# Residual loaded ahead of the products, a third score bank and a new plan in a two-layer decoder trunk

## The chip, the cores and the metric

One core of a Trainium2 chip runs the whole kernel. The metric is the device time of one execution in microseconds. Before the change three runs took 1709.66 to 1713.77 us, with a median of 1711.59 us.

## The reference

The input is x of 2048 positions and 1024 channels in float32. All of it is float32.

```python
# layer 0: gated short convolution
h = rmsnorm(x, norm_a)
B, C, X, G = split(h @ w_in_a, 4)                       # 1024 -> 4 x 1024
y = B * causal_conv3(C * X, conv_a)
x = x + (y * silu(G)) @ w_out_a                         # 1024 -> 1024
# keys and values, once
k, v = split(rmsnorm(x, norm_kv) @ w_kv, 2)             # 8 heads of 64
# layer 1: stick-breaking attention, strictly causal
q, g = split(rmsnorm(x, norm_b) @ w_in_b, 2)
z = q k^T / 8
rev = reverse_cumsum(where(mask, log_sigmoid(-z), 0))   # from the last key backwards
o = exp(where(mask, z + rev, -inf)) @ v
x = x + (o * silu(g)) @ w_out_b                         # 512 -> 1024
return rmsnorm(x, norm_f)
```

## The kernel before

**Layout.** The activations lie transposed, channels on the 128 partitions and positions, last one first, along the free axis, in four chunks c = 0 to 3 of 512 positions. A block is one tile of 128 channels by 512 positions. Every float32 operand of a product is split in a high part (rounded) and a low part (the rest), and a product is three matmuls of these parts (hi·hi, hi·lo, lo·hi).

**Stages.** First the mixer's input products for two blocks of channels, directly (`mixer_in`), then for the rest, two chunks at a time, by Strassen-like units of seven products in place of eight (`fast_unit`): fa, fd and fe are its three PSUM banks, from the tags lin (two banks), z and wt; a product is 12 matmuls of 512 columns. The output products of mixer A follow in the same form, four units of two blocks for chunks 0 and 1 and four for chunks 2 and 3 (`out_unit`, tiles named _o). Then come the K, Q, V and gate products for chunks 0 and 1 as units (kq, vg), and for chunks 2 and 3 directly (pk, pq, pv, pg), the attention of 4 chunks by 8 heads, the output projection (pob) with the final norm, and, for chunk 3, an end (`finish`) that waits for the last head: its last part of the output product (pol), the norm and the store.

**A unit's banks.** In `fast_unit` fa collects a first product; a copy f1 of it is kept, the next product is added onto the bank, and so on, so that the bank passes through several partial sums. Three of these states (f1 and f2 of fa, f5 of fd) are copied by ScalarE to SBUF tiles of the tag ld (5 buffers); TensorE may only go on in the bank once the copy is done. VectorE then adds the other banks onto the copies. The fourth result stays in fa. In `out_unit`, after that, each of the four results gets its residual: a block of x is loaded (tag t, 4 buffers), the result is added onto it (GpSimd for the first block, VectorE for the others), the sum is stored to x1 in HBM, squared by ScalarE and added to a running sum by GpSimd.

**Norms.** The squares are added block by block to one tile; `rstd` sums it over the partitions by matmuls with a column of ones (pst) and takes the root by three steps of Newton on 128 x 4 numbers. `bcast` spreads this factor over the partitions: VectorE multiplies it into four identity matrices (dg) and TensorE multiplies ones by it in float32 (prb). Both tiles come from a bank of their own, tag st.

**Attention.** For each head and chunk of keys: four score tiles (z, 128 queries by 512 keys, two matmuls each, tag z with two banks), a sigmoid on ScalarE, a running product along the keys on VectorE (the scan), transposes on TensorE to a wt bank (two), a split into wth and wtl, and two matmuls with the values into av. The eight PSUM banks are lin 2, z 2, wt 2, av 1, st 1.

**Order.** All instructions are recorded (class `Recorder`), each in a part (mixer unit, output unit, head of a chunk, ...), and put in order before the program is built: PLAN gives each part a start and an end, which become a priority of each of its instructions; then a list scheduler with costs for each engine, buffers and transfers takes the one that can begin first, and among equals the one of the smaller priority. Every engine runs its instructions in that order, and waits in it. Loads and stores are issued from SyncE's queue (SP), keys, values and queries of the attention from ScalarE's.

## Time and profile before

| | us |
|---|---|
| median of the runs | 1711.59 |
| profiled execution | 1716.8 |
| its span, first to last instruction | 1715.0 |
| TensorE busy | 1640.0 |
| VectorE busy | 1346.2 |
| ScalarE busy | 802.3 |
| GpSimd busy | 542.7 |

The profile is of one execution. PE is TensorE's matmuls, PEld its weight loads, DVE VectorE, ACT ScalarE, POOL GpSimd, SPq the queue of SyncE. Since an instruction of TensorE overlaps the next one, a matmul of 512 columns shows about 0.39 us but a row of 12 takes 2.72 us. In a row of the timeline stand the start, the time, engine, operation, output and inputs, and in brackets the idle time before it and what ended it. A row of busy time by stretch has the stretch, its length, then the busy time of PE, PEld, DVE, ACT and POOL with the count of instructions, the granted clock of TensorE, the share of the DMA engines and GB/s. Nearly all instructions carry line 353, from which all recorded ones are issued, so they are told apart by their tiles.

### The profile page before, as it was taken

What the parts mean: (1) busy time and instruction counts of PE and PEld (TensorE: products, weight loads), DVE (VectorE), ACT (ScalarE), POOL (GpSimd) and SP (SyncE); (2) the same over time, 40 slices, a digit from 0 to 9 for tenths busy, and PEclk for the clock granted to TensorE, in tenths of its full rate; (3) what the DMA queues carried; (4) which work ended last, traced back from release to release, by engine and by line L of the source; (5) the groups of instructions that cost most, each with busy time, mean ns of one, the idle gap of its engine ahead of it and who ended that gap; (6) DMA issues with size and microseconds to landing.
All of it is one profiled execution on the core that took longest, in us unless ns stands there. A gap on an engine that the chain in (4) does not pass through costs nothing.

```text
span 1715.0 us, 23851 instructions
## 1 busy us (share of the span) xinstructions
PE 1640.0 (96%) x7784; PEld 1332.8 (78%) x7784; DVE 1346.2 (78%) x1951; ACT 802.3 (47%) x1505; POOL 542.7 (32%) x715
## 2 busy tenths in 40 slices
PE   7999999999999999998799999999999999999995
PEld 5878887888888887776577877878888787888874
DVE  6998678864636369776887777888999789989896
ACT  6444344521313134533544454556565566656552
POOL 5340000100000004366642232234433145646743
PEclk9999999999999999999999999999999999999998
DMA  9478797887362669997577999778676797789953
GB/s 270 166 234 305 251 305 266 290 307 228 90 196 86 209 221 328 348 321 261 175 245 270 308 330 284 223 220 251 221 217 184 244 313 241 229 253 305 290 165 133
DMA packets 256972, 419.49 MB, mean 245 GB/s; under 512 B 21072, under 2 KB 135760, under 8 KB 256848
## 3 DMA queue, kind: packets, MB, share of 16 engines
q1 hardware_dynamic: 196768, 359.20, 62.7%
q10 hardware_dynamic: 59920, 58.74, 12.3%
q8 instruction: 62, 1.02, 0.2%
q14 instruction: 62, 0.51, 0.1%
q0 software_dynamic: 160, 0.02, 0.1%
HBM read 265.06 MB, written 152.83 MB: 244 GB/s over the span
## 4 chain that ended last, share of the span: by engine, by line
PE 70%; DVE 12%; DMA 9%; issue 4%; ACT 3%; POOL 1%; ACTq 0%; SPq 0%; POOLq 0%; DVEq 0%
PE fa_C L353 8%; PE fa_B L353 8%; PE av L353 7%; PE z L353 6%; PE wt L353 6%; PE fd_B L353 4%; PE fd_C L353 4%; PE pob L353 3%; PE fa_o L353 3%; PE pv L353 3%; PE pg L353 2%; PE fa_kq L353 2%; PE pk L353 2%; PE pq L353 2%; PE fe_C L353 2%
## 5 line engine op out<-in xcount | busy, mean ns | idle before, releaser
L353 DVE TENSOR_TENSOR_SCAN R<-R,cy,ones 128x512 f32<-128x512 f32 x192 | 248.4, 1320 | 2.6 <-ACT R L353 2.4
L353 ACT CAST wth<-wt 128x512 fp32r<-128x512 f32 (+3 forms) x320 | 155.2, 525 | 180.5 <-PE wt L353 134.6
L353 DVE TENSOR_TENSOR wtl<-wt,wth 128x512 fp32r<-128x512 f32 (+1 forms) x320 | 181.7, 600 | 41.5 <-ACT wth L353 34.2
L353 PE MATMUL z<-kt,q 128*128 128x512 f32 (+2 forms) x640 | 188.7, 383 | 6.3 <-ACT R L353 4.9
L353 ACT ACTIVATE R<-z 128x512 f32<-128x512 f32 (+1 forms) x320 | 162.6, 543 | 57.2 <-PE z L353 50.5
L353 PE MATMUL wt<-ident,R 128*128 128x128 f32 x1088 | 171.9, 274 | 1.3 <-DVE R L353 1.3
L353 POOL COPY halo<-p 128x2 f32<-128x2 f32 x32 | 17.1, 533 | 459.4 <-DVE p L353 419.0
L353 PEld LDWEIGHTS wt<-ident,R 128*128 128x128 f32 x1088 | 135.5, 142 | 24.9 <-DVE R L353 3.3
L353 POOL COPY cy<-R 128x1 f32<-128x1 f32 x192 | 107.4, 560 | 144.3 <-DVE R L353 121.4
L353 PEld LDWEIGHTS z<-kt,q 128*128 128x128 f32 x640 | 110.6, 190 | 27.5 <-ACT R L353 10.8
L353 PE MATMUL av<-wth,vv 128*128 128x512 f32 (+1 forms) x320 | 121.1, 379 | 9.4 <-ACT wth L353 6.4
L353 PE MATMUL av<-wtl,vv 128*128 128x512 f32 (+1 forms) x320 | 124.2, 392 | 1.1 <-DVE wtl L353 1.1
L353 DVE TENSOR_TENSOR_SCAN R<-R,ones 128x256 f32<-128x256 f32 (+3 forms) x128 | 103.5, 838 | 4.1 <-POOL R L353 3.1
L353 PE MATMUL pob<-og,whl_ob 128*128 128x512 f32 x360 | 103.0, 401 | 0.6 <-ACT og L353 0.3
L353 POOL TENSOR_SCALAR_AFFINE_SELECT R<-R 128x128 f32<-128x128 f32 x128 | 65.4, 519 | 114.6 <-ACT R L353 111.9
L353 POOL TENSOR_TENSOR acc_x<-acc_x,sq_x 128x512 f32<-128x512 f32 x51 | 74.2, 1455 | 73.0 <-ACT sq_x L353 71.4
L353 PEld LDWEIGHTS av<-wth,vv 128*128 128x128 f32 x320 | 60.3, 189 | 31.3 <-ACT wth L353 14.7
L353 PE MATMUL fa_C<-op_t,whl_s_C 128*128 128x512 f32 x336 | 82.8, 389 | 0.0
L353 PE MATMUL fa_B<-op_t,whl_s_B 128*128 128x512 f32 x336 | 81.3, 389 | 0.0
L353 PEld LDWEIGHTS pob<-og,whl_ob 128*128 128x128 f32 x360 | 65.5, 188 | 13.2 <-ACT og L353 0.8
L353 PEld LDWEIGHTS av<-wtl,vv 128*128 128x128 f32 x320 | 60.6, 189 | 17.5 <-DVE wtl L353 4.6
L353 PEld LDWEIGHTS fa_B<-op_t,whl_s_B 128*128 128x128 f32 x336 | 63.0, 188 | 13.5 <-DVE whl_s_B L353 0.4
(582 smaller groups left out, 3793.2 us busy)
## 6 DMA issues: line engine op xcount, KB each, us to landing
kt<-k_d ACTq DMA_DIRECT2D x80, 256.0 KB, 4.5
vv<-v_d ACTq DMA_DIRECT2D x80, 256.0 KB, 4.6
q<-q_d ACTq DMA_DIRECT2D x64, 256.0 KB, 5.9
sw_s_C<-whl_s_C SPq DMA_DIRECT2D x24, 512.0 KB, 4.0
sw_s_B<-whl_s_B SPq DMA_DIRECT2D x24, 512.0 KB, 3.6
whl_s_C<-sw_s_C SPq DMA_DIRECT2D x24, 512.0 KB, 4.4
whl_s_B<-sw_s_B SPq DMA_DIRECT2D x24, 512.0 KB, 4.4
whl_ob<-sw_ob SPq DMA_DIRECT2D x24, 512.0 KB, 5.3
```

The costliest lines, as they stand in the source:

```text
L353: getattr(o.engine.engine, o.name)(*map(real, o.args), **{k: real(v) for k, v in o.kw.items()})
```

## The change

It has six pieces.

1. `out_unit` hands `fast_unit` its own `keep`. It loads the residual block into a tile of the tag ld ahead of time and lets VectorE add the bank onto it; so the three copies by ScalarE and the later adds onto the residual go. The fourth result still gets its residual, in a tile of the tag t, after the unit.
2. The bank of the tag st goes and the scores get a third one (NZ 2 to 3). The tiles of the norms take a bank of the tag wt, which the transposed weights and fe use.
3. `bcast` uses four transposes of the factor's columns, spread over 128 columns by a stride of zero, and no diagonal tile.
4. `norm_1` copies the spread factor to SBUF and multiplies by that.
5. In `finish` the squares of each of the eight blocks are summed over the partitions on TensorE, onto one small tile, with no adds on GpSimd and VectorE, and the factor is spread twice, into two banks, one for ScalarE's copy and one for VectorE.
6. The values are stored with the two heads of a block apart, so that a load of one head reads one run for each partition. And PLAN has new numbers throughout.

```diff
-NLIN, NZ, NWT, NAV = 2, 2, 2, 1
+NLIN, NZ, NWT, NAV = 2, 3, 2, 1
 PLAN = {
-    "m01": (-1194.8, -595.9), "x0": (-582.3, -466.4), "x1": (-1592.9, -1402.4), "s2": (-160.0, -8.6),
+    "m01": (-1662.9, -893.2), "x0": (-957.0, -706.9), "x1": (-1431.4, -1360.8), "s2": (-179.7, 4.9),
...
-    v_d = [[dram.tile([P, 4, 2, 2, 64], F32, name=f"v_d_{c}_{h}") for h in range(NH // 2)] for c in range(NCH)]
+    v_d = [[dram.tile([P, 2, 4, 2, 64], F32, name=f"v_d_{c}_{h}") for h in range(NH // 2)] for c in range(NCH)]
...
     def st(nm):
-        return psum.tile([P, CH], F32, name=nm, tag="st", bufs=1)
+        return psum.tile([P, CH], F32, name=nm, tag="wt", bufs=NWT)
...
     def bcast(y, nm):
         pb = st(f"prb_{nm}")
-        dg = sb.tile([P, 4, P], F32, name=f"dg_{nm}", tag="t", bufs=NT)
-        nc.vector.tensor_mul(dg, y.unsqueeze(2).to_broadcast([P, 4, P]), ident.unsqueeze(1).to_broadcast([P, 4, P]))
-        nc.tensor.matmul(pb, ones, dg.rearrange("p j i -> p (j i)"), start=True, stop=True)
+        for j in range(4):
+            nc.tensor.transpose(pb[:, j * P:(j + 1) * P], y[:, j:j + 1].to_broadcast([P, P]), ident)
         return pb
...
-    def fast_unit(c, nm, w):
+    def fast_unit(c, nm, w, keep=None):
...
-        def keep(n, ps):
+        def copy(n, ps):
             t = ld512(f"{n}_{nm}")
             nc.scalar.copy(t, ps)
             return t
+        keep = keep or copy
...
-        for i, both in enumerate(fast_unit(("o", c), nm, w)):
-            for j, r in enumerate(both):
+        def residual(i, j):
+            ob = 2 * u + j
+            x = (t512 if i == j == 1 else ld512)(f"x1_{c + i}_{ob}")
+            nc.sync.dma_start(out=x, in_=xT[ob * P:(ob + 1) * P, cols(c + i)])
+            return x
+
+        def keep(n, ps):
+            x = residual(*{"f1": (1, 0), "f5": (0, 1), "f2": (0, 0)}[n])
+            nc.vector.tensor_add(x, x, ps)
+            return x
+
+        for i, both in enumerate(fast_unit(("o", c), nm, w, keep)):
+            for j, x in enumerate(both):
                 ob = 2 * u + j
-                x = t512(f"x1_{c + i}_{ob}")
-                nc.sync.dma_start(out=x, in_=xT[ob * P:(ob + 1) * P, cols(c + i)])
-                (nc.gpsimd if i == j == 0 else nc.vector).tensor_add(x, x, r)
+                if i == j == 1:
+                    r, x = x, residual(i, j)
+                    nc.vector.tensor_add(x, x, r)
                 nc.sync.dma_start(out=x1_d[c + i][ob], in_=x)
...
     def norm_1(c):
-        pb = bcast(r1[c], f"x1{c}")
+        rs = sb.tile([P, CH], F32, name=f"rs1_{c}", tag="acc", bufs=2)
+        nc.scalar.copy(rs, bcast(r1[c], f"x1{c}"))
...
-            nc.vector.tensor_mul(x, x, pb)
+            nc.vector.tensor_mul(x, x, rs)
...
     def finish(c):
+        ps2 = psum.tile([P, CH], F32, name=f"pst_x2{c}", tag="wt", bufs=NWT)
         for ob in range(KD):
             ps = lin(f"pol_{ob}")
             mm3(ps, [wl[ob // 4][:, :, ob % 4:ob % 4 + 1, :]], og[3:4], kt=1)
             nc.vector.tensor_add(x2[ob], x2[ob], ps)
...
-        pb = rstd_bcast(acc[1], f"x2{c}")
+            sq = sb.tile([P, CH], F32, name=f"sq_x2{c}{ob}", tag=("wth", "wtl")[ob % 2], bufs=NWTS)
+            nc.scalar.activation(sq, x2[ob], AF.Square)
+            for j in range(4):
+                nc.tensor.matmul(ps2[:, j:j + 1], sq[:, j * P:(j + 1) * P], ones[:, 0:1], start=ob == j == 0, stop=ob == KD - 1 and j == 3,
+                                 skip_group_check=True)
+        y = rsqrt(ps2, f"x2{c}")
         pbs = t512(f"pbs_{c}")
-        nc.scalar.copy(pbs, pb)
+        nc.scalar.copy(pbs, bcast(y, f"x2{c}s"))
+        pb = bcast(y, f"x2{c}")
```

How this moves instructions, at three places:

ScalarE before, in the second half of the output units: f_o is a bank's kept state, sq_x the square of a finished block x_c_ob, x_2_3 the block of chunk 2, channels 3.

```order
L353 COPY f_o_2_6818<-fa_o_2_6790 128x512
L353 CAST whl_a_kq_6843<-fr_a_kq_6171 128x512
L353 CAST whl_s_kq_6850<-fr_a_kq_6195 128x512
L353 COPY r1s<-prb_x_6854 128x512
L353 ACTIVATE sq_x_6865<-x_2_2_6772 128x512
L353 ACTIVATE sq_x_6898<-x_2_3_6809 128x512
L353 COPY f_o_2_6902<-fa_o_2_6790 128x512
L353 CAST whl_s_kq_6921<-fr_a_kq_6171 128x512
L353 CAST op_b_kq_6933<-xb_kq_6426 128x512
```

The last copy f_o (third unit) stands behind the squares of the second unit's blocks x_2_2 and x_2_3. Now the bank is taken by VectorE; there, for the fourth unit (fa_o_2_6940, fd_o_2_6969):

```order
L353 TENSOR_TENSOR x_3_6_6890<-x_3_6_6890,fa_o_2_6940 128x512
L353 TENSOR_TENSOR x_3_5_6921<-x_3_5_6921,fa_o_2_6723 128x512
L353 TENSOR_TENSOR x_2_7_6914<-x_2_7_6914,fd_o_2_6969 128x512
L353 TENSOR_TENSOR fr_a_kq_6470<-fr_a_kq_6470,fr_a_kq_6178 128x512
L353 TENSOR_TENSOR xb_kq_6639<-xb_kq_6571,xb_kq_6639 128x512
L353 TENSOR_TENSOR xb_kq_6702<-xb_kq_6578,xb_kq_6702 128x512
L353 TENSOR_TENSOR xb_kq_6708<-xb_kq_6626,xb_kq_6708 128x512
L353 TENSOR_TENSOR xb_kq_6546<-xb_kq_6772,xb_kq_6546 128x512
L353 TENSOR_TENSOR x_2_6_6964<-x_2_6_6964,fa_o_2_6940 128x512
```

Its three keeps (onto x_3_6, x_2_7 and x_2_6) stand among the operands of the K and Q units, and behind the fourth block of the third unit, x_3_5, whose residual is loaded late.

SyncE's queue before, where the residuals of the fourth unit's last blocks (x_3_6, x_3_7) are asked for; whl_s_o and whl_a_o are the unit's weights, k_d and q_d the stores of keys and queries, fr_a_vg the weights of a value and gate unit:

```order
L353 DMA x_d_6_149<-x_2_6_7092 128x512
L353 DMA fr_a_vg_7407<-in_w_in_b_dram 128x4x128
L353 DMA k_d_0_167<-khl_0_0_7389 64x512
L353 DMA k_d_1_168<-khl_0_0_7389 64x512
L353 DMA fr_a_vg_7422<-in_w_kv_dram 128x4x128
L353 DMA k_d_0_159<-khl_0_1_7430 64x512
L353 DMA k_d_1_160<-khl_0_1_7430 64x512
L353 DMA k_d_4_171<-khl_2_0_7448 64x512
L353 DMA x_3_6_7455<-in_xT_dram 128x512
L353 DMA x_3_7_7460<-in_xT_dram 128x512
```

Now, the same residual x_3_7 and its neighbours:

```order
L353 DMA whl_s_o_2_6938<-sw_s_o_0_418 128x1024
L353 DMA x_2_6_6964<-in_xT_dram 128x512
L353 DMA sw_kv_4_424<-whl_a_kq_6976 128x1024
L353 DMA whl_s_o_2_6996<-sw_s_o_0_419 128x1024
L353 DMA x_d_5_156<-x_3_5_6921 128x512
L353 DMA fr_a_kq_7015<-in_w_in_b_dram 128x4x128
L353 DMA whl_a_o_2_7024<-sw_a_o_0_420 128x1024
L353 DMA x_3_7_7041<-in_xT_dram 128x512
L353 DMA whl_s_o_2_7045<-sw_s_o_0_421 128x1024
L353 DMA whl_a_o_2_7072<-sw_a_o_0_422 128x1024
```

x_3_7 is asked for between the weights of its own unit (sw_a_o_0_420, sw_s_o_0_421), and x_3_6 nine rows ahead of this piece.

TensorE at the end before:

```order
L353 MATMUL pol_17446<-og_3_17398,whl_obl_17263 128x512 x3
L353 MATMUL pol_17455<-og_3_17398,whl_obl_17263 128x512 x3
L353 MATMUL pol_17462<-og_3_17398,whl_obl_17263 128x512 x3
L353 MATMUL pst_x_17480<-ones,acc_x_1_17431 128x1 x4
L353 MATMUL prb_x_17502<-dg_x_17500,ones 128x512
```

and now, from the fifth block on (pst_x the sums of squares, one row is four matmuls of one column; prb the spread factor):

```order
L353 MATMUL pol_17427<-og_3_17353,whl_obl_17178 128x512
L353 MATMUL pst_x_17392<-ones,sq_x_17420 128x1 x4
L353 MATMUL pol_17427<-og_3_17353,whl_obl_17178 128x512 x2
L353 MATMUL pol_17438<-og_3_17353,whl_obl_17178 128x512
L353 MATMUL pst_x_17392<-ones,sq_x_17434 128x1 x4
L353 MATMUL pol_17438<-og_3_17353,whl_obl_17178 128x512 x2
L353 MATMUL pol_17450<-og_3_17353,whl_obl_17178 128x512 x3
L353 MATMUL pst_x_17392<-ones,sq_x_17448 128x1 x4
L353 MATMUL pst_x_17392<-ones,sq_x_17460 128x1 x4
L353 MATMUL pst_x_17392<-ones,sq_x_17462 128x1 x4
L353 MATMUL prb_x23s<-ident,yr_x_17477 128x128 x4
L353 MATMUL prb_x_17493<-ident,yr_x_17477 128x128 x4
```

One sum behind the last product has become eight, most of them between the products, and each spread is four transposes.

More of the change, by code (lines that the diff above doesn't have):

```diff
@@ L445, in rstd, with rsqrt @@
                 nc.tensor.matmul(ps[:, j:j + 1], a[:, j * P:(j + 1) * P], ones[:, 0:1], start=i == 0, stop=i == len(acc) - 1)
+        return rsqrt(ps, nm, y)
+    def rsqrt(ps, nm, y=None):
         v = sb.tile([P, 4], F32, name=f"v_{nm}", tag="sv")
@@ L983, in out_v @@
             nc.tensor.transpose(pt[:, b * P:(b + 1) * P], t[:, b * P:(b + 1) * P], ident)
-        vt = sb.tile([P, 4, 2, 2, 64], F32R, name=f"vt_{c}_{vb}", tag="hl", bufs=1)
-        split(vt[:, :, :, 0, :], vt[:, :, :, 1, :], pt.rearrange("p (b h d) -> p b h d", b=4, d=64))
+        vt = sb.tile([P, 2, 4, 2, 64], F32R, name=f"vt_{c}_{vb}", tag="hl", bufs=1)
+        split(vt[:, :, :, 0, :], vt[:, :, :, 1, :], pt.rearrange("p (b h d) -> p h b d", b=4, d=64))
         nc.sync.dma_start(out=v_d[c][vb], in_=vt.bitcast(F32))
@@ L1025, in attention @@
             vt = sb.tile([P, 4, 2, 64], F32R, name=f"vv_{nm}", tag="vv" if own else "wraw", bufs=2 if own else NRAW)
-            nc.scalar.dma_start(out=vt.bitcast(F32), in_=v_d[kc][hb][:, :, hi_, :, :])
+            nc.scalar.dma_start(out=vt.bitcast(F32), in_=v_d[kc][hb][:, hi_, :, :, :])
             ws = []
@@ L1158, in finish @@
         og = og_t[c]
-        acc = [sb.tile([P, CH], F32, name=f"acc_x2{c}_{i}", tag="acc", bufs=2) for i in range(2)]
+        ps2 = psum.tile([P, CH], F32, name=f"pst_x2{c}", tag="wt", bufs=NWT)
         for ob in range(KD):
@@ L1163, in finish @@
             nc.vector.tensor_add(x2[ob], x2[ob], ps)
-            if ob < 2:
-                nc.scalar.activation(acc[ob], x2[ob], AF.Square)
-            else:
-                sq = t512(f"sq_x2{c}{ob}")
-                nc.scalar.activation(sq, x2[ob], AF.Square)
-                if ob in (2, 4):
-                    nc.gpsimd.tensor_add(acc[0], acc[0], sq)
-                else:
-                    nc.vector.tensor_add(acc[1], acc[1], sq)
-                if ob == 6:
-                    nc.vector.tensor_add(acc[1], acc[1], acc[0])
-        pb = rstd_bcast(acc[1], f"x2{c}")
+            sq = sb.tile([P, CH], F32, name=f"sq_x2{c}{ob}", tag=("wth", "wtl")[ob % 2], bufs=NWTS)
[4 more added lines that the diff above has]
+        y = rsqrt(ps2, f"x2{c}")
         pbs = t512(f"pbs_{c}")
-        nc.scalar.copy(pbs, pb)
+        nc.scalar.copy(pbs, bcast(y, f"x2{c}s"))
+        pb = bcast(y, f"x2{c}")
         for k in range(KD):
```

44 rows, old and new, of the table PLAN are left out of this document.

## The prediction

> **What bounds the kernel now.** I read first the page, then the busy time by stretch, then TensorE's waits, then the rows of a few waits.
>
> ```profile
> span 1715.0 us, 23851 instructions
> PE 1640.0 (96%) x7784; PEld 1332.8 (78%) x7784; DVE 1346.2 (78%) x1951; ACT 802.3 (47%) x1505; POOL 542.7 (32%) x715
> ...
> 588.00:637.00 49.00, 49.00 (x218) 40.55 (x217) 26.54 (x41) 14.65 (x26) 2.94 (x7) 1.00 0.66 211
> 637.00:784.00 147.00, 138.20 (x596) 110.61 (x595) 118.26 (x169) 66.60 (x118) 72.14 (x50) 0.99 0.96 335
> 784.00:931.00 147.00, 128.77 (x544) 99.59 (x544) 116.54 (x169) 67.65 (x119) 71.14 (x59) 0.98 0.67 222
> 980.00:1666.00 686.00, 668.53 (x3564) 550.56 (x3563) 605.16 (x829) 393.94 (x805) 288.10 (x476) 0.99 0.80 251
> ```
>
> TensorE is the bound: in 588 to 637 us (mixer) it has no idle time at all. It idles 75 us in the span: 8.8 in 637 to 784 (output products of mixer A), 18.2 in 784 to 931 (last output products and the first K, Q, V, G products), 17.5 in 980 to 1666 (projections, attention, output projection), and most of the rest at start and end. VectorE is busy 80% of 637 to 931 and 88% of the attention; the DMA engines are full (0.96) only in 637 to 784. So a saving on TensorE counts nearly in full, one on another engine only where TensorE waits for it. What TensorE waits for in 640 to 935 us:
>
> ```profile
> PE fa_o L353 <- DVE x L353: 8.2, 4, 3.0
> PE fa_o L353 <- ACT f_o L353: 6.1, 2, 3.4
> ...
> PE fa_o L353 <- DVE f_o L353: 1.6, 2, 0.8
> ...
> PE fd_o L353 <- ACT f_o L353: 0.7, 1, 0.7
> ```
>
> 16.6 of 27.0 us of idle time are four forms of one wait: a bank of an output unit has not been evacuated (f_o) or released (x). One of them, in order of time:
>
> ```profile
> 787.49 0.74 SPq L353 DMA_DIRECT2D x<-in_xT_dram  x1
> 792.76 0.63 ACT L353 ACTIVATE sq_x<-x 128x512 f32<-128x512 f32 x1 [4.25 <-DMA x<-in_xT_dram]
> 793.30 0.57 ACT L353 COPY f_o<-fa_o 128x512 f32<-128x512 f32 x1
> 793.92 0.50 PE L353 MATMUL fa_o<-op_t_('o', 2)_0_6409,whl_s_o 128*128 128x512 f32 x1 [2.70 <-ACT f_o L353]
> ...
> 795.20:798.60 3.40, 3.15 (x8) 1.94 (x6) 0.21 (x1) 0.21 (x1) 2.57 (x3) 0.51 0.84 333
> ```
>
> The residual of one unit is asked for late (787.49) and lands after 792. The square of that block waits for it on ScalarE, and behind the square, in the same queue, stands the copy of the next unit's bank, for which TensorE waits 2.70 us. Right after such a wait the granted clock is 0.51 for 3.4 us, so a window of that kind costs up to another 1.7 us.
>
> **Residual first.** Per output unit the change drops three ScalarE copies, two VectorE adds of two SBUF operands and a GpSimd add; instead VectorE adds three banks onto residuals that are already loaded.
>
> ```profile
> L353 ACT COPY f_o<-fa_o x16: 567/587/589, 649.0 to 823.5; 128x512 f32<-128x512 f32 x16
> L353 DVE TENSOR_TENSOR x<-x,f_o x16: 683/866/1777, 676.1 to 874.8; 128x512 f32<-128x512 f32 x16
> L353 DVE TENSOR_TENSOR f_o<-f_o,fd_o x8: 675/681/687, 665.2 to 824.2; 128x512 f32<-128x512 f32 x8
> L353 POOL TENSOR_TENSOR x<-x,f_o x8: 1293/1678/1747, 666.0 to 855.4; 128x512 f32<-128x512 f32 x8
> ```
>
> VectorE had four adds from PSUM (0.68) and two from SBUF (0.87), 4.45 us a unit; it will have seven from PSUM, 4.76 us. Over eight units that is +2.5 us for VectorE, minus 24 x 0.59 = 14 us for ScalarE and 8 x 1.68 = 13 us for GpSimd, none of it on the path by itself. What counts is the waits: the copy no longer stands behind a square that waits for a transfer. In its place VectorE's add now waits for its own residual, behind VectorE's other rows, so some of the wait moves rather than goes. The fourth block of a unit (both indices 1) still loads its residual at the end and keeps its bank until then. Yet at one place that is far better than before:
>
> ```profile
> 835.67 0.39 PE L353 MATMUL fa_o<-op_t_('o', 2)_3_6761,whl_a_o 128*128 128x512 f32 x1
> ...
> 869.77 1.50 SPq L353 DMA_DIRECT2D x<-in_xT_dram  x2
> ...
> 875.51 0.68 DVE L353 TENSOR_TENSOR x<-x,fa_o 128x512 f32<-128x512 f32 x1
> ```
>
> Before, the last two residuals of the stage were asked for 34 us after the last output matmul, behind the K and Q stores, and one of the two "lin" banks was held for 40 us. In the new order both stand among the unit's own weight loads. Bounds of the whole part: no gain, or 16.6 us of waits and three half-clock windows (5.1; the one shown is the second of them), 21.7 us. I take 7: somewhat under half of the waits, since VectorE (80% busy) takes over the evacuation and the DMA engines stay full.
>
> **Norm factor by transposes.** Twelve times VectorE built a diagonal tile and TensorE multiplied it in float32.
>
> ```profile
> 785.28 0.69 DVE L353 TENSOR_TENSOR dg_x<-r,ident 128x512 f32<-128x512 f32 x1
> 786.33 1.02 PE L353 MATMUL prb_x<-dg_x,ones 128*128 128x512 f32 x2
> ...
> 1660.71 0.60 PE L353 MATMUL wt<-ident,R 128*128 128x128 f32 x4
> ```
>
> The two passes take 1.02 us to the end of the second, four transposes 0.60; so 0.42 us of TensorE each time. The one at the end is costed below; the other eleven give 11 x 0.42 = 4.6, of which I take 4, since a few stand in stretches where TensorE waits anyway. VectorE loses 12 x 0.69 = 8 us and the dependent chain 0.7 us each, hidden behind other matmuls. In the two norms of the residual ahead of the projections, the factor is copied to SBUF first: two more copies (0.59), and 16 multiplies go from a PSUM operand to two SBUF operands, at 0.87 against 0.68 at most 16 x 0.19 = 3 us of VectorE, about what the residual part adds; both are paid by the 8 us.
>
> **Third score bank.** The own bank of the norms goes; scores get a third one.
>
> ```profile
> PE av L353 <- ACT wth L353: 6.4, 8, 2.2
> PE z L353 <- ACT R L353: 4.9, 10, 1.1
> PE av L353 <- DMA vv<-v_d: 2.7, 2, 2.0
> ...
> 1030.80:1034.20 3.40, 3.40 (x11) 2.78 (x10) 2.46 (x5) 1.03 (x3) 0.00 (x0) 0.50 0.96 300
> ```
>
> The scores' own wait is 4.9 us in 686: the ceiling, with perhaps three half-clock windows (the one shown and two more like it) at 1.7 us, is 10. Against it the norms' tiles now take turns with the transposed weights on two banks, and the wait of the weighted sum for its copies (6.4) is on that very pair; on the losing side I allow 5. I take a gain of 2, nearer to the score wait's own row.
>
> **Values' layout.** Each partition of a value load becomes one run of 2 KB in place of four of 512 B. The wait that could shrink is 2.7 us, in two places; I take 0.2.
>
> **The end.**
>
> ```profile
> 1687.69 7.15 PE L353 MATMUL pol<-og,whl_obl 128*128 128x512 f32 x24
> ...
> 1698.65 1.05 PE L353 MATMUL pst_x<-ones,acc_x 128*128 128x1 f32 x8 [3.82 <-DVE acc_x L353]
> 1699.74 0.16 DVE L353 TENSOR_SCALAR v_x<-pst_x 128x4 f32<-128x4 f32 x1 [1.15 <-PE pst_x L353]
> ...
> 1702.12 0.69 DVE L353 TENSOR_TENSOR dg_x<-yr_x,ident 128x512 f32<-128x512 f32 x1
> 1702.96 2.05 PE L353 MATMUL prb_x<-dg_x,ones 128*128 128x512 f32 x2 [3.25 <-DVE dg_x L353]
> 1705.04 0.59 ACT L353 COPY pbs<-prb_x 128x512 f32<-128x512 f32 x1 [8.01 <-PE prb_x L353]
> 1705.66 3.38 DVE L353 SCALAR_TENSOR_TENSOR x<-x,g_f,prb_x 128x512 f32<-128x512 f32 x5 [2.85 <-ACT pbs L353]
> ```
>
> It looks as if the sums of squares got faster: the 3.82 us wait for the adders goes. But eight sums in place of one are 64 small matmuls, at 1.05 us for eight, of which I count 0.93 until the next can start, 7.4 us in all, between 24 product matmuls, of which three take 0.68. TensorE becomes the bound of the end: from the third product (about 1690.0) 5 x 0.68 + 8 x 0.93 = 10.8 us, so the last sum is there at about 1700.9, and the root's first step starts at 1701.05, 1.3 us later than now. The twelve steps of the root then take the same 2.4 us (1699.74 to 1702.12, where the diagonal starts). Behind them the diagonal (0.69 and its handover) and the 2.05 us of passes go, for two sets of four transposes in two banks; the first is there some 0.85 us after the root, the second 0.5 later, and VectorE no longer waits for ScalarE's copy of the same bank. VectorE starts at 1704.8 in place of 1705.66. Gain 0.8; bounds 4.4 (if the small matmuls hide under the eight adds) and a loss of 1.5.
>
> The Trainium skill, "TensorE: Matmul & The Clock Gate", section "Part 4: PE-mode transpose", says that a transpose does not count as work for the clock gate. By it the last eight transposes would run at half clock and take about 0.9 us more, so the end would gain nothing and the sum below would be 13.2; the trace has granted 0.50 at 1703 to 1706 already, but with a product in that place, so no row of it shows this.
>
> **New plan.** Every row moves; no row of this trace prices it. I take 0, with bounds of 10 us each way: somewhat over half of what TensorE idles in 784 to 931 (18.2) or in 980 to 1666 (17.5).
>
> **Sum.** 7 + 4 + 2 + 0.2 + 0.8 + 0 = 14.0 us. The profiled execution is 1716.8 us (span 1715.0), so it would become 1702.8. The median of the runs shown is 1711.59, 5.2 under it; the same difference gives 1697.6 us.
>
> **Rivals.** (1) *The residual's round trip paces the units; slower.* Three of the five "ld" buffers are now held by a unit from the load to the store, where before they were held only from the copy to the add.
>
> ```profile
> 713.30 2.72 PE fd_o L353 x12
> ...
> x<-in_xT_dram SPq DMA_DIRECT2D x32, 256.0 KB, 5.5
> x_d<-x SPq DMA_DIRECT2D x32, 256.0 KB, 5.0
> ...
> DMA to landing us min/median/max: 2.2/5.0/8.3
> ```
>
> A unit is seven products of 2.72, 19.0 us. Its sixth buffer request, the third residual of the next unit, is needed 19.0 + 8.2 = 27.2 us after a unit's start and can go only when the first store has landed; that block is complete at 10.9. In these 16.3 us lie an add and handovers (1.0), a store (5.0) and a load (5.5), with about 0.7 for the issue: 4.1 us to spare. It decides when the two landings together pass 14.6 us; two at 8.3 are 16.6. Then each of the six units behind a first one loses 2 us, three of them with a half-clock window: 12 + 5.1, and the 7 us of gain fall away: 1711.6 - 7 + 17.1 = 1721.7. For it: the DMA engines are full there, and all loads share SP's queue. Against it: units overlap, and the medians leave room. Chance 0.17. (2) *Hidden anyway.* VectorE or the full DMA engines set the pace, TensorE's waits come back under other names, and of the sum only half the transposes stay: 1711.6 - 2 = 1709.6. For it: 0.96 DMA share and 80% VectorE in the stage; the same bytes. Against it: 784 to 931 idles twice as much at a share of 0.67. Chance 0.15. (3) *The stage is cured.* All waits and windows of the first part go, and the plan fills another 5: 1711.6 - 14 - 14.7 - 5 = 1678. Chance 0.13.
>
> **How the numbers follow.** My forecast, 1697.6 us, has 0.55, with 1688 to 1707 as its own range. The range over the cases is 1680 to 1717: it leaves out the far halves of (1) and (3). A measurement here can tell about 0.2%, 3.4 us, so faster means under 1708.2 and slower over 1715.0. Faster: 0.53 + 0.13 + 0.04 of (2) = 0.70. Same: 0.02 + 0.10 + 0.01 = 0.13. Slower: 0.16 of (1) and 0.01 of (2), 0.17.
>
> **What would show it.** Right: TensorE's waits for f_o gone and those for x under 10 us in the output stage, no half-clock window there, four transposes of 0.60 for each factor, fewer waits of z, the root's first step 13 to 14 us ahead of the end. Wrong: waits of fa_o for VectorE's adds that themselves wait for a residual (1); idle time of the same size with weights or operands as releasers (2); losses in the attention where there were none (the plan).

## The result and the profile after

The changed kernel took 1685.79 us (median of four runs, 1684.09 to 1690.13), the kernel before, beside it, 1712.68 us: a ratio of 0.9844, with a 95% interval of 0.9812 to 0.9875. That is 26.9 us less. The forecast was 1697.6, 14 less; the time lies inside the range of 1680 to 1717, and just below the forecast's own 1688 to 1707. The profiled execution took 1685.95 us (1716.8 before), so the two traces differ by 30.9 us. Here are the span and the busy times of the changed kernel, and then its busy time by the same stretches as before:

```profile
span 1684.2 us, 23924 instructions
...
PE 1631.7 (97%) x7868; PEld 1345.1 (80%) x7868; DVE 1339.4 (80%) x1942; ACT 788.5 (47%) x1483; POOL 514.2 (31%) x705
```

```profile
637.00:784.00 147.00, 142.75 (x623) 114.38 (x621) 116.49 (x179) 58.30 (x100) 74.12 (x50) 0.99 0.97 348
784.00:931.00 147.00, 136.07 (x588) 108.69 (x587) 120.73 (x175) 69.72 (x124) 64.08 (x55) 0.98 0.70 232
980.00:1666.00 686.00, 673.94 (x3660) 564.84 (x3658) 623.24 (x841) 396.96 (x812) 287.08 (x478) 1.00 0.78 250
```

TensorE idles less in each: 4.3 us instead of 8.8, 10.9 instead of 18.2, 12.1 instead of 17.5. VectorE is about as busy as before (237 us of 637 to 931, 235 before), and the DMA engines are as full (0.97 in 637 to 784). To see where the time went, I cut both traces at the same work rather than the same time: at the start of the first product of an output unit (fa_o), of the last one, and of the last weighted sum (av). The busy time of these two middle stages, first before and then after:

```profile
643.30:835.70 192.40, 173.00 (x726) 136.30 (x724) 147.94 (x204) 82.81 (x146) 98.28 (x70) 0.97 0.88 303
835.70:1681.10 845.40, 818.98 (x4234) 669.84 (x4233) 735.16 (x1018) 467.81 (x935) 354.09 (x533) 0.99 0.79 249
```

```profile
641.40:819.10 177.70, 167.75 (x721) 133.76 (x720) 139.48 (x207) 71.63 (x122) 90.00 (x64) 0.98 0.93 333
819.10:1646.20 827.10, 809.22 (x4254) 673.09 (x4253) 742.92 (x1016) 465.32 (x936) 337.73 (x528) 1.00 0.77 251
```

| us | mixer | output stage | from there to the last av | end | span |
|---|---|---|---|---|---|
| before | 643.3 | 192.4 | 845.4 | 33.9 | 1715.0 |
| after | 641.4 | 177.7 | 827.1 | 38.0 | 1684.2 |
| difference | -1.9 | -14.7 | -18.3 | **+4.1** | -30.8 |

So the result is not the forecast with a better size: one stage gains twice its 7 us, the long one gains 18 where 6 were summed, and the end, forecast 0.8 shorter, is 4.1 longer. TensorE's waits in 640 to 935 us of the changed kernel:

```profile
PE fa_kq L353 <- DVE x L353: 4.0, 2, 3.7
PE fa_kq L353 <- DVE op_t_kq L353: 3.3, 3, 1.7
PE fa_o L353 <- DVE x L353: 2.3, 3, 0.8
PE fa_kq L353 <- ACT op_t_kq L353: 1.4, 2, 1.1
```

The waits for f_o are gone, and those for the residual's adds (x) are 6.3 us in place of 8.2. The largest one left, in order of time:

```profile
796.00 1.52 DVE L353 TENSOR_TENSOR op_b_kq<-xb_kq,op_b_kq 128x512 fp32r<-128x512 f32 x1
796.18 0.39 PE L353 MATMUL fd_o<-op_t_('o', 2)_3_6330,whl_s_o 128*128 128x512 f32 x1
796.94 1.48 POOL L353 TENSOR_TENSOR fr_a_kq<-fr_a_kq,g_b 128x512 f32<-128x512 f32 x1
797.45 1.52 DVE L353 TENSOR_TENSOR whl_a_kq<-fr_a_kq,whl_a_kq 128x512 fp32r<-128x512 f32 x1
798.89 1.27 DVE L353 TENSOR_TENSOR x<-x,fa_o 128x512 f32<-128x512 f32 x2
...
800.31 2.90 PE L353 MATMUL fa_kq<-op_b_kq,whl_a_kq 128*128 128x512 f32 x6 [3.74 <-DVE x L353]
```

TensorE has finished the unit's products and wants the bank of fa_o for the first K and Q unit; VectorE, which now empties that bank, is still busy with two operands of the K and Q units. This is the wait that "moves rather than goes". From 799.7 on the clock is granted at half for 3.4 us, as behind such waits before.

### The profile page after: what moved, and what is told of

The parts are those of the page before. It is cut to its first block, busy times and chain, and to the rows that moved or that the text cites. A ratio compares the mean times of both kernels' runs of the same rounds, so it can differ in the third digit from the quotient of the medians.

```text
span 1684.2 us, 23924 instructions
## 1 busy us (share of the span) xinstructions
PE 1631.7 (97%) x7868; PEld 1345.1 (80%) x7868; DVE 1339.4 (80%) x1942; ACT 788.5 (47%) x1483; POOL 514.2 (31%) x705
## 3 DMA queue, kind: packets, MB, share of 16 engines
q8 instruction: 62, 1.02, 0.3%
## 4 chain that ended last, share of the span: by engine, by line
PE 72%; DVE 9%; DMA 6%; issue 3%; ACT 2%; POOL 1%; ACTq 0%; POOLq 0%; SPq 0%; DVEq 0%
PE fa_C L353 9%; PE fa_B L353 9%; PE av L353 6%; PE z L353 6%; PE wt L353 5%; PE fd_C L353 4%; PE fd_B L353 4%; PE fa_o L353 4%; PE pob L353 3%; DVE R L353 3%; PE pk L353 2%; PE pg L353 2%; PE fe_C L353 2%; PE fd_o L353 2%; PE pq L353 2%
## 5 line engine op out<-in xcount | busy, mean ns | idle before, releaser
L353 DVE TENSOR_TENSOR wtl<-wt,wth 128x512 fp32r<-128x512 f32 (+2 forms) x320 | 180.3, 596 | 24.7 <-ACT wth L353 23.8
L353 PE MATMUL z<-kt,q 128*128 128x512 f32 (+2 forms) x640 | 181.3, 379 | 2.9 <-DMA q<-q_d 1.8
L353 ACT ACTIVATE R<-z 128x512 f32<-128x512 f32 (+2 forms) x320 | 159.1, 547 | 43.4 <-PE z L353 36.2
L353 PE MATMUL wt<-ident,R 128*128 128x128 f32 x1088 | 165.7, 272 | 0.8 <-DVE R L353 0.8
L353 POOL COPY cy<-R 128x1 f32<-128x1 f32 x192 | 93.7, 490 | 144.4 <-DVE R L353 129.7
L353 POOL TENSOR_SCALAR_AFFINE_SELECT R<-R 128x128 f32<-128x128 f32 x128 | 72.9, 584 | 95.5 <-ACT R L353 93.3
L353 PEld LDWEIGHTS fa_C<-op_t,whl_s_C 128*128 128x128 f32 x336 | 62.9, 188 | 15.4 <-DVE op_t L353 2.4
```

The costliest lines, as they stand in the source:

```text
L353: getattr(o.engine.engine, o.name)(*map(real, o.args), **{k: real(v) for k, v in o.kw.items()})
```

## The experiments

Ratios are to the kernel before, run beside each kernel on the same chip (medians there 1711.71 to 1713.55 us); they stand with their 95% intervals. The stages are those of the one profiled execution of each kernel, cut as above; it can lie some us off the median (jitter's took 1697.63, struct_only's 1716.52). How much a stage moves by itself can be read from five kernels whose order is the same up to the end (after, old_values, end_adds, wide_sums, wide_five): 177.6 to 180.1 in the output stage, 824.3 to 830.0 in the long one.

| us | runs' median | ratio | mixer | output stage | to last av | end |
|---|---|---|---|---|---|---|
| before | 1712.68 | 1 | 643.3 | 192.4 | 845.4 | 33.9 |
| after | 1685.79 | 0.9844 (0.9812 to 0.9875) | 641.4 | 177.7 | 827.1 | 38.0 |
| plan_only | 1732.56 | 1.0124 (1.0104 to 1.0144) | 644.1 | 197.7 | 856.8 | 35.1 |
| struct_only | 1711.57 | 1.0002 (0.9985 to 1.0019) | 648.6 | 186.8 | 841.5 | 37.8 |
| resid_only | 1705.90 | 0.9957 (0.9937 to 0.9976) | 642.7 | 185.4 | 841.0 | 35.9 |
| jitter | 1702.91 | 0.9938 (0.9917 to 0.9959) | 640.3 | 176.7 | 844.2 | 34.3 |
| jitter2 | 1702.15 | 0.9939 (0.9919 to 0.9958) | 640.3 | 188.2 | 839.9 | 35.4 |
| residual_late | 1709.08 | 0.9982 (0.9969 to 0.9995) | 639.9 | 194.6 | 839.4 | 34.5 |
| two_z | 1698.27 | 0.9911 (0.9887 to 0.9934) | 640.3 | 178.3 | 841.6 | 35.3 |
| diag_bcast | 1693.29 | 0.9885 (0.9868 to 0.9901) | 642.4 | 176.8 | 833.3 | 40.5 |
| old_values | 1687.63 | 0.9845 (0.9816 to 0.9874) | 640.0 | 178.3 | 830.0 | 33.3 |
| end_adds | 1681.46 | 0.9828 (0.9809 to 0.9847) | 641.4 | 180.1 | 825.5 | 33.6 |
| wide_sums | 1680.73 | 0.9824 (0.9806 to 0.9842) | 640.8 | 177.6 | 824.3 | 34.6 |
| wide_five | 1676.64 | 0.9785 (0.9758 to 0.9812) | 641.6 | 178.5 | 825.1 | 31.4 |

**Structure or numbers.** The first two runs take the change apart along its broadest seam.

```diff
 # plan_only: the kernel before
-PLAN = { the old numbers }
+PLAN = { the new numbers }
 # struct_only: the changed kernel
-PLAN = { the new numbers }
+PLAN = { the old numbers }
```

> The kernel before with nothing but the new PLAN numbers. The change took 28 to 31 us in all: by stretches of the two traces 14.7 between the first and last output product, 18.3 from there to the last weighted sum, 1.9 in the mixer, and the end is 4.1 longer. Theory 1 (structure): the numbers alone bring the old banks, copies and residuals at most 5 us either way, 1707 to 1717 us, and TensorE's waits for f_o and for the residual's adds in the output stage stay at 13 us or more. Theory 2 (numbers): most of the 18.3 us behind the output stage comes with them: 1695 us or less, of which the output stage itself keeps its 192 us. A third way: numbers that fit other buffers do harm, over 1720 us.

> The changed kernel with the old PLAN numbers: all five changes of structure, none of the order's. Theory 1 (structure): it keeps the 14.7 us of the output stage and the third score bank's share, and loses the end's 4: 1688 to 1698 us. Theory 2 (numbers): it keeps little, 1705 us or more, with the same waits as before under other names. The one-column sums at the end must cost the same 4 us here as in the changed kernel, since they do not depend on the numbers.

Neither theory holds in both runs. The numbers alone make the old kernel 21 us slower (1.0124; the third way that was named for it), the structure alone leaves the time where it was (1.0002), and both together save 27. Neither part has a worth of its own that could be added to the other's. Struct_only shows why its zero is a sum: its output stage is 5.5 us shorter, the next stretch 3.9, but the end is 3.9 longer and the mixer, which the structure hardly touches, 5.3. The mixer's loss is a new wait and the half clock behind it:

```profile
336.66 0.49 PE L353 MATMUL fa_C<-op_t,whl_s_C 128*128 128x512 f32 x1 [1.57 <-ACT op_t L353]
337.88 0.73 PE L353 MATMUL fa_C<-op_t,whl_s_C 128*128 128x512 f32 x2 [0.72 <-DVE op_t L353]
339.79 5.78 PE L353 MATMUL fa_B<-op_t,whl_s_B 128*128 128x512 f32 x12 [1.18 <-ACT whl_s_B L353]
```

A row of twelve takes 5.78 there, against 2.88 in the kernel before at the same place. The list scheduler had ordered the mixer anew: TensorE's rows differ from the kernel before from 39 us on, at the first spread of a norm factor. Which of its picks led to this wait was not traced.

**The price of another order.** Two draws move each number of PLAN by at most 0.3 us and change nothing else.

```diff
 # jitter, jitter2: the changed kernel
-    "m01": (-1662.9, -893.2), ...
+    "m01": (-1662.9, -893.3), ...   # jitter: every number moved by a random -0.3 to +0.3
```

> The changed kernel with each number of PLAN moved at random by at most 0.3 us; nothing else. It prices a reordering as such, since the undone parts and the old numbers of the other runs reorder nearly every row too. Theory A (the numbers are a rough guide): within 4 us of the changed kernel, 1682 to 1690 us. Theory B (each set of numbers was fitted to one structure, and any other order costs, as the 21 us that the new numbers cost the old structure and the 26 us that the new structure loses with the old numbers suggest): 8 us or more above it, 1694 to 1712 us, the loss spread over the stages.

> The changed kernel with each number of PLAN moved at random by at most 0.3 us once more, by another draw. In the first draw the mixer and the output stage kept their times (640.3 and 176.7 us) and the stretch from the last output product to the last weighted sum went from 827.1 to 844.2, where the kernel before has 845.4. Theory (the 18 us of that stretch are the fit of this one order, not the third bank or the other pieces): 836 us or more in it again, the output stage at 175 to 182. Rival (the first draw was unlucky): 832 or less.

Theory B holds, both times: 0.9938 and 0.9939, which is 10.5 us under the kernel before, but 16 over the changed one. In the first draw the output stage keeps its gain (176.7) and the long stretch loses all of it (844.2, with 845.4 before); in the second the stretch loses 12.8 and the output stage 10.5, outside the 175 to 182 that I had expected. So the loss of the first draw is not spread over the stages, as theory B had it. The first draw's two stages:

```profile
640.30:817.00 176.70, 166.54 (x721) 131.36 (x720) 141.74 (x206) 71.80 (x122) 92.37 (x65) 1.00 0.94 332
817.00:1661.20 844.20, 815.57 (x4256) 672.71 (x4255) 739.72 (x1017) 464.79 (x935) 338.92 (x527) 1.00 0.76 247
```

Beside the rows of after, TensorE idles 28.6 us in the long stretch in place of 17.9, and is 6.4 busier with the same matmuls. Two rows of its waits in 960 to 1655 us carry most of what came back, first the changed kernel (960 to 1640), then the draw:

```profile
PE av L353 <- DVE wtl L353: 4.3, 7, 1.5
PE av L353 <- ACT wth L353: 3.1, 5, 1.2
...
PE z L353 <- ACT R L353: 0.6, 2, 0.4
```

```profile
PE av L353 <- ACT wth L353: 9.7, 12, 1.9
PE av L353 <- DVE wtl L353: 3.7, 6, 1.1
PE z L353 <- ACT R L353: 2.6, 3, 1.5
```

So the fit of this one order to the chip is worth about 16 us against these two draws, and 10.5 us are left for the structure under an order that is not fitted. That comparison is lopsided: the numbers of the kernel before were not shifted, so whether its time holds a like fit is open. Plan_only is the old structure under numbers not made for it, and the draws lie 30 us below it; the structure is worth 10.5 or 30 us, depending on which of the two it is compared with.

**Residual first, alone and undone.**

```diff
 # resid_only: the kernel before, with out_unit and fast_unit of the change
+        def keep(n, ps):
+            x = residual(*{"f1": (1, 0), "f5": (0, 1), "f2": (0, 0)}[n])
+            nc.vector.tensor_add(x, x, ps)
+            return x
...
 # residual_late: the changed kernel, with the old out_unit
-        for i, both in enumerate(fast_unit(("o", c), nm, w, keep)):
+        for i, both in enumerate(fast_unit(("o", c), nm, w)):
...
+                x = t512(f"x1_{c + i}_{ob}")
+                nc.sync.dma_start(out=x, in_=xT[ob * P:(ob + 1) * P, cols(c + i)])
+                (nc.gpsimd if i == j == 0 else nc.vector).tensor_add(x, x, r)
```

> The kernel before with the first piece of the change alone: residuals loaded first, banks added onto them by VectorE; old banks, old numbers. So far the stage from the first to the last output product took 192 to 198 us in the three kernels with the old output units and 177 to 187 in the seven with the new ones, whatever the numbers. Theory: 178 to 188 us in that stage, f_o's waits gone, the rest dearer by the price of a reordering (0 to 17 us behind the stage): 1698 to 1718 us in all. Rival (the new units need the new numbers or the third bank): 190 us or more in the stage.

> The changed kernel with the output units of before: copies by ScalarE, the residuals loaded at the end, adds on VectorE and GpSimd. From the first to the last output product the kernel before took 192.4 us and the changed one 177.7. Theory (residual first is what shortened that stage): 188 us or more in it, f_o back among TensorE's waits there, and the rest of the kernel within 5 us; 1696 to 1702 us in all. Rival (the numbers did it): the stage within 4 us of 177.7, and f_o's waits under 3 us. If every stage is longer by some us, it is the price of a reordering, to be read against the run with moved numbers.

The old output units took 192.4, 197.7 and 194.6 us in their stage, the new ones 176.7 to 188.2 in eleven kernels: no kernel crosses. Alone, the piece shortens its stage by 7.0 us, to 185.4 as the theory had it, and the kernel by 7.4 (0.9957; 4 to 11). Undone in the changed kernel, it costs 16.9 in the stage, as the theory had it, and 24 in all, above the range of 1696 to 1702: the long stretch behind has 12.3, within what another order cost in the draws. f_o came back among the waits, but with 2.9 us, which by my own mark of 3 speaks for the rival; the waits that carry the loss are others:

```profile
PE fa_o L353 <- DVE x L353: 8.7, 3, 4.1
PE fe_o L353 <- DMA whl_a_o<-sw_a_o: 4.3, 1, 4.3
PE fd_o L353 <- DMA whl_s_o<-sw_s_o: 3.5, 1, 3.5
PE fa_o L353 <- DVE f_o L353: 2.2, 2, 1.4
```

Twice the weights themselves are late, for 7.8 us. They share SyncE's queue with the late residuals, and the DMA engines are busy at 0.87 in this stage; why they are late only under this order was not tried.

**Third score bank, transposes, values.** Three pieces are undone one at a time in the changed kernel.

```diff
 # two_z
-NLIN, NZ, NWT, NAV = 2, 3, 2, 1
+NLIN, NZ, NWT, NAV = 2, 2, 2, 1
-        return psum.tile([P, CH], F32, name=nm, tag="wt", bufs=NWT)
+        return psum.tile([P, CH], F32, name=nm, tag="st", bufs=1)
 # diag_bcast
-        for j in range(4):
-            nc.tensor.transpose(pb[:, j * P:(j + 1) * P], y[:, j:j + 1].to_broadcast([P, P]), ident)
+        nc.vector.tensor_mul(dg, y.unsqueeze(2).to_broadcast([P, 4, P]), ident.unsqueeze(1).to_broadcast([P, 4, P]))
+        nc.tensor.matmul(pb, ones, dg.rearrange("p j i -> p (j i)"), start=True, stop=True)
 # old_values
-    v_d = [[dram.tile([P, 2, 4, 2, 64], ...
+    v_d = [[dram.tile([P, 4, 2, 2, 64], ...
...
```

> The changed kernel with two score banks and a bank of its own for the norms' tiles, as before. From the last output product to the last weighted sum the kernel before took 845.4 us and the changed one 827.1. Theory (the third bank is worth a few us): TensorE's waits of z for ScalarE's R back at 4 to 6 us, 2 to 6 us more in that stretch. Rival 1 (the bank is most of the 18.3): 12 us or more in that stretch with z's waits as the largest. Rival 2 (it is worth nothing, the waits were covered): within 2 us. The output stage stays as it is up to the price of a reordering.

> The changed kernel with the diagonal tile and the float32 product for every spread of a norm factor. Theory: 11 times 0.42 us of TensorE, 4 to 5 us, and at the end two diagonals (0.69 each) and two products of 2.05 at half clock in place of two sets of transposes, some 2 us: 6 us in all, with the waits unchanged. Rival (hidden beside other waits): under 2 us. More than 10 us would be the price of a reordering, not of the spread.

> The changed kernel with the values stored as before, the two heads of a block side by side, so that a load of one head reads four pieces of 512 B in each partition instead of one of 2 KB. All engines keep the order of the changed kernel. Theory: the loads' queue moves about twice as many packets (29200 against 59920 in the two pages), the waits of the weighted sum for its values grow by at most 2.7 us: 0 to 3 us more than the changed kernel. Rival (the shorter transfers are part of the 18 us of the attention): 5 us or more.

Two_z costs 11.5 us (0.9911 against 0.9844), its profiled execution has 14.5 more in the long stretch, and z's waits for R are back at 4.3 us, though not as the largest: those of the weighted sum for wth are 7.7. So none of the three expectations fits: the loss is the size of rival 1 without its wait. The two draws, which have the third bank, cost 16, with z's waits at 2.6 and 1.3. The bank takes some 2 to 4 us of waits away (4.3 against 2.6, 1.3 and the changed kernel's 0.6), and its share of the total can't be told from the price of another order. Diag_bcast costs 7 us, near the 6 that were expected; it too carries a reordering, so the 7 support the sum from rows and don't prove it. They also show that not every other order costs 16: this one differs from 39 us on, and its dearer spreads are in the 7. Old_values is the one clean undo: TensorE, VectorE, ScalarE, GpSimd and SyncE keep their order. It changes nothing (0.9845 against 0.9844), though the packets of the values' queue double, after and old_values:

```profile
q10 hardware_dynamic: 29200, 58.74, 11.9%
```

```profile
q10 hardware_dynamic: 59920, 58.74, 12.5%
```

**The end.** The changed kernel's last 30 us on TensorE (pol the last output products, pst the sums of squares, of which each x8 is one block in two passes), and then the granted clock of two stretches of it:

```profile
1652.34 2.61 PE L353 MATMUL pol<-og,whl_obl 128*128 128x512 f32 x9
1654.79 0.95 PE L353 MATMUL pst_x<-ones,sq_x 128*128 128x1 f32 x8
...
1659.10 0.97 PE L353 MATMUL pst_x<-ones,sq_x 128*128 128x1 f32 x8
1659.93 1.63 PE L353 MATMUL pol<-og,whl_obl 128*128 128x512 f32 x3
1661.36 1.70 PE L353 MATMUL pst_x<-ones,sq_x 128*128 128x1 f32 x8
1662.92 2.48 PE L353 MATMUL pol<-og,whl_obl 128*128 128x512 f32 x5
1665.20 5.11 PE L353 MATMUL pst_x<-ones,sq_x 128*128 128x1 f32 x24
1672.84 1.09 PE L353 MATMUL prb_x23s<-ident,yr_x 128*128 128x128 f32 x4 [2.52 <-DVE yr_x L353]
```

```profile
1655.00:1659.90 4.90, 4.90 (x38) 4.59 (x38) 2.05 (x3) 3.47 (x6) 2.33 (x2) 1.00 0.55 191
1659.90:1670.40 10.50, 10.41 (x42) 9.56 (x41) 2.11 (x4) 2.99 (x5) 0.00 (x0) 0.50 0.00 0
```

TensorE has no idle time in the 4.9 us before, and still its clock falls to 0.50 in the middle of the sums. From the first product to the end of the last sum pass 18.0 us. Three kernels ask why, and what a better end is worth.

```diff
 # end_adds: the changed kernel; squares added on VectorE and GpSimd, one sum at the end, as before
-            for j in range(4):
-                nc.tensor.matmul(ps2[:, j:j + 1], sq[:, j * P:(j + 1) * P], ones[:, 0:1], ...)
+                if ob in (2, 4):
+                    nc.gpsimd.tensor_add(acc[0], acc[0], sq)
+                else:
+                    nc.vector.tensor_add(acc[1], acc[1], sq)
...
 # wide_sums: the changed kernel
-                nc.tensor.matmul(ps2[:, j:j + 1], sq[:, j * P:(j + 1) * P], ones[:, 0:1], ...)
+                nc.tensor.matmul(ps2[:, j, :], sq[:, j * P:(j + 1) * P], ones, ...)
...
 # wide_five: wide_sums, and
+            if ob in (0, 2, 4):
+                first = sq
+                continue
+            if ob in (1, 3, 5):
+                (nc.vector if ob == 5 else nc.gpsimd).tensor_add(sq, sq, first)
```

> The changed kernel with the squares of the end added on VectorE and GpSimd again and one sum of eight small matmuls, the spread by transposes into two banks kept. The instructions ahead of the end keep their order. In the changed kernel 31.9 us pass from the first product of the last part (1652.3) to the end, against 27.3 before, and from 1659.9 on the clock is 0.50 while TensorE has no idle time. Theory (the sums cost the end): from the first product to the end 25.5 to 27, the clock 1.0 until the last product is done, 5 us less in all: about 1681 us. Rival (the end is set by handovers and stores, and the sums lie beside them): 30 us or more from the first product to the end, 1684 to 1687 us.

> The changed kernel with each of its one-column sums made 128 columns wide (ones as the moving operand, so that every column holds the same sum; the root reads one of each 128): the same count of small matmuls and of weight loads, 128 times the columns. It tells what makes the clock fall. Theory (columns streamed: with one column TensorE is busy in the records yet almost idle for the clock): the clock stays at 1.0 until the last sum is done, four sums in two passes take 1.0 to 1.2 us, and the root starts 14 to 16 us behind the first product in place of 18.1; 2 to 4 us less than the changed kernel. Rival (the weight loads or the alternation of shapes make it fall): half clock from the same place, and the wide sums take 2 us each, 1 to 6 us more than the changed kernel.

> The changed kernel with an end between the two: the squares of blocks 0 and 1, 2 and 3 added in pairs by GpSimd, of 4 and 5 by VectorE, those of 6 and 7 alone, so five sums in place of eight, each 128 columns wide as in the run with wide sums. All else keeps its order. Theory (with the clock kept the end is as long as TensorE's products plus its sums): 6.7 of products, five sums of 1.0, so 12 to 13 us from the first product to the last sum, against 14.7 with eight wide sums and 18.1 with eight narrow ones: 1 to 2.5 us less than with eight wide sums, about 1679 us. Rival (the adds or the squares of the last blocks end last): no gain over eight, 1680 to 1683 us.

Wide_sums has the same count of small matmuls with 128 times the columns. Its four runs (1679.12 to 1682.44) lie below the four of the changed kernel (1684.09 to 1690.13), though the intervals of the two ratios overlap; in the traces its end is 3.3 us shorter. Its TensorE at the end, and the clock of the stretch with the last sums:

```profile
1656.66 2.84 PE L353 MATMUL pst_x<-ones,sq_x 128*128 128x128 f32 x24
1659.26 1.39 PE L353 MATMUL pol<-og,whl_obl 128*128 128x512 f32 x5
1661.41 2.05 PE L353 MATMUL pst_x<-ones,sq_x 128*128 128x128 f32 x16 [0.76 <-ACT sq_x L353]
```

```profile
1656.00:1663.50 7.50, 6.70 (x49) 5.75 (x47) 2.33 (x5) 4.09 (x7) 0.00 (x0) 1.00 0.00 0
```

Three wide sums take 2.84 us where three narrow ones took 5.11, and the clock is 1.0 until the last sum is done, though TensorE idles more (0.8 us in that stretch). The scheduler, which counts a wide sum as dearer, put some of the sums in other places between the products; the count of weight loads and the alternation stayed. So idle time, weight loads and alternation don't explain the fall; what is left is the one column. Old_values adds a nuance. It has the order of the changed kernel, and in its profiled execution the same narrow sums ran through at full clock:

```profile
1661.70:1667.70 6.00, 6.00 (x45) 5.56 (x44) 2.06 (x3) 3.33 (x5) 0.00 (x0) 1.00 0.00 0
```

There 13.3 us pass from the first product to the last sum, and the end takes 33.3. The clock falls at 1667.71, just as the last sum ends. Over the eight profiled kernels with narrow sums, that time is 13.3 to 18.0 us, and the clock falls 5.0 to 11.0 us after the first sum; in the other seven 0.8 to 10.6 us of sums and products still follow. In the two kernels with wide sums it falls 2.5 and 4.1 us after the last sum.

The traces also show when it falls. In each of these ten kernels all changes to half clock lie a whole number of steps of 3.41 us apart. Cut back from the fall in such steps, this is the share of a step in which TensorE was busy with products of 512 columns, from the step of the first sum on:

| | step by step | the clock then |
|---|---|---|
| after | 0.78, 0.44 | falls, 10.4 us before the last sum is done |
| old_values | 0.86, 0.55, 0.61, 0.22 | falls as the last sum ends |
| wide_sums | 0.78, 0.59, 0.33, 0.41 | is kept, and falls one step later, in which only the last 0.9 us of sums lie |
| wide_five | 0.81, 0.41, 0 | is kept (the step with 0 is 0.79 busy with wide sums), and falls one step later, which has transposes alone |

In all eight kernels with narrow sums the step before the fall has 0.22 to 0.56 of products, and the steps that kept the clock have 0.55 or more. With wide sums, steps of 0.33, 0.41 and 0 kept it. So the narrow sums hardly count as work for the clock and the wide ones do, and how much an execution loses, up to 4.7 us, goes with where the steps fall among its sums and products: old_values was lucky in that, not better.

End_adds gives 33.6 for the end and 27.5 from the first product, 0.5 over the expected range; its TensorE waits 4.66 us for the adders, as the kernel before did for 3.82. Wide_five joins both: five sums, at full clock, with little waiting.

```profile
1657.21 1.16 PE L353 MATMUL pst_x<-ones,sq_x 128*128 128x128 f32 x8 [0.36 <-POOL sq_x L353]
1658.13 1.41 PE L353 MATMUL pol<-og,whl_obl 128*128 128x512 f32 x5
1659.70 3.84 PE L353 MATMUL pst_x<-ones,sq_x 128*128 128x128 f32 x32 [0.17 <-POOL sq_x L353]
1666.07 0.62 PE L353 MATMUL prb_x23s<-ident,yr_x 128*128 128x128 f32 x4 [2.52 <-DVE yr_x L353]
```

12.3 us from the first product to the last sum (12 to 13 expected), an end of 31.4 (34.6 with eight wide sums, a gain above the 1 to 2.5 us expected), and 1676.64 us in all. Its six runs (1673.77 to 1680.47) lie below the four of the changed kernel (1684.09 to 1690.13): it is the fastest kernel of this study.

## Why the prediction was right, and where not

**The number.** The time lies inside the stated range, and that is partly luck. The sum left the order out, which gave 16 us against the draws; the structure gave 10.5 there in place of 14, and the end lost where a gain was summed. The range reached down to 1680 for another reason, a cured output stage.

**What bounds the kernel.** Right: of the 33 us that the two middle stages gained, 18 are idle time of TensorE (19.4 to 9.9 us and 26.4 to 17.9). The rest is time in which it shows as busy: three half-clock windows fewer (1.7 us each), the transposes (0.42 us for each of seven spreads there) and the spacing of the same matmuls.

**Residual first, 7 us.** Right as a term: alone it gave 7.0 in its stage and 7.4 in all. In the changed kernel the stage gained 14.7, within the bounds of 0 to 21.7; the other half came with the order: it is there in one draw (176.7) and gone in the other (188.2) and under the old numbers (186.8). The mechanism is the one described, with its second half too: the waits for f_o are gone, and some of the wait moved behind VectorE's other rows (the 3.74 us at 800.31). One of its signs was wrong: I had asked for no half-clock window in the stage, and there are two (680.3 and 799.7) in place of three.

**Norm factor by transposes, 4 us.** Four transposes take the 0.60 us that were forecast, against 1.02:

```profile
1533.32 0.60 PE L353 MATMUL prb_x<-ident,yr_x 128*128 128x128 f32 x4
```

The undo cost 7 us, with two spreads at the end and a reordering in it; the term is supported, its size not separated.

**Third score bank, 2 us.** z's waits for R went from 4.9 to 0.6 us, as forecast; how much of that reached the end is not settled.

**Values' layout, 0.2 us.** Right: nothing measurable.

**New plan, 0 us.** This is the step that failed. It was taken as zero because no row prices it, with 10 us each way. It measured about 16 us, beyond its bound, as the difference of the changed kernel to the two draws. What share of the kernel before is such a fit, no run shows. The bound came from half the idle time of one stretch; the order changed the idle time of both, and the time of the same matmuls besides (6.4 us in the first draw's long stretch). The error in the thinking lay deeper: the plan was treated as one more term. The four kernels of old and new structure and numbers (1, 1.0124, 1.0002, 0.9844) show that it has no value apart from the structure that it was made for. The forecast of 14 for the rest stands against 10.5 for the structure under a plan that is slightly off.

**The end, 0.8 us gained.** Wrong in the profiled execution, by 4.9 us and beyond its bound of 1.5 lost, and wrong in its reason: 13.2 us from the first product to the last sum were worked out at the full clock, from the 1.05 us of a sum in the trace of before. With the clock kept (old_values) the time is 13.3 and the end 0.6 shorter, so the arithmetic held; what it left out is that the clock falls under these very sums. My sign for it, a root 13 to 14 us ahead of the end, came true (1670.35, 13.8) and proved nothing: it was measured from the wrong side of the loss.

```profile
1670.35 0.16 DVE L353 TENSOR_SCALAR v_x<-pst_x 128x4 f32<-128x4 f32 x1 [4.22 <-PE pst_x L353]
```

The Trainium skill ("TensorE: Matmul & The Clock Gate", "Part 4: PE-mode transpose") says that a transpose does not count as busy for the clock gate in the way a matmul does. The last eight did run at half clock here (1.09 for four), but the clock had fallen 13 us earlier; in wide_five they took 0.62 at full clock. So these traces neither bear the rule out nor contradict it. The loss came from the sums ahead of them.

**The rivals.** The round trip of the residuals did not pace the units: VectorE's adds waited for a residual twice, for 2.7 us in all; before, they waited as long in five places.

```profile
DVE x L353 <- DMA x<-in_xT_dram: 2.7, 2, 1.9
```

"Hidden anyway" is refuted by resid_only, where the residual part alone reached the end with 7.4 us. The cured stage with 5 us from the plan, at 1678, was too large for the stage and the end and too small for the plan; the time lies between it and the forecast.

## What to carry to other kernels

When a scheduler orders the program, a change of structure and a change of its numbers are one change: run each alone, and run a small random shift of the numbers, on the kernel before as well, before a gain or a loss is put down to either. A single undo with a reordering in it says little; a piece can be priced where the order stays (old_values, the ends), or by the one stage that it touches over many orders (the output units). Before small matmuls go onto a busy TensorE, look at what the granted clock does under them; here making them 128 times as wide made the end shorter.

## What was not expected of the hardware

The clock fell under one-column matmuls though TensorE's records show no idle time: 4.90 us busy of 4.90 ahead of 1659.9, and 0.50 from there on. The same sums with 128 columns kept 1.00 up to 1663.5; eight passes took 1.05 us, narrow ones 0.95 at full clock. And a shift of 0.3 us in the plan's numbers, in a kernel of 1686 us, moves the time by 16 us; in the first draw's long stretch that is 10.7 us of idle time, in waits of at most 1.9 us each, and 6.4 us in which the same matmuls show as busy for longer.
